# Gate and up products of a SwiGLU FFN by one level of Strassen's algorithm, and no sums of SBUF tiles on GpSimd

## The chip, the cores and the metric

One Trainium2 chip, one of its cores. The metric is the device time of one execution in microseconds (us), lower is better; the time before is the median of three runs. TensorE is written PE, its weight loads PEld, VectorE DVE, ScalarE ACT, GpSimd POOL, and the queue from which the loads are issued SP.

## The reference

A trunk of two layers on 512 tokens of width 1024, all in f32. Each layer is a token mixer (layer 0: forgetting attention and sparse attention; layer 1: differential attention), a cross attention to 256 memory tokens, and a SwiGLU FFN of inner width 2816, each between two RMS norms with a residual. What the change touches is the FFN:

```python
def swiglu(h, wg, wu, wd):
    return (jax.nn.silu(h @ wg) * (h @ wu)) @ wd
...
        y = swiglu(rms_norm(x, g[4]), ffn_wg[layer], ffn_wu[layer], ffn_wd[layer])
        x = x + rms_norm(y, g[5])
```

## The kernel before

**Splitting.** Every f32 operand of a large product is kept as a high part in the float32r type and a low part, the rest. `split` makes them from a source: an ACT copy writes the high part, a DVE subtraction the low part. `mm` then issues three matmuls for one 128-row block of the contraction: high by high, high by low, low by high.

**FFN (`ffn`).** The inner width of 2816 is cut into 22 chunks of 128 columns. `up(c)` loads 512 KB of the gate weights and 512 KB of the up weights (tiles `raw`, 3 buffers), splits each into two tiles `w` (8 buffers), and for each of the two weights issues 8 `mm`, one per 128 rows of the contraction: the weights are the stationary operand, and the transposed tokens `hT` (high and low, `[128, 8, 512]`) stream by, 512 columns to a matmul. That is 48 matmuls for a chunk; for the first two chunks they come in two halves of 256 tokens (96 matmuls), since the last token blocks are late. Then silu and the product: `th` by ACT's tanh, two `scalar_tensor_tensor` of DVE, and a split of the result into `acts[c]`, whose low part is a subtraction on GpSimd. The down product takes groups of three chunks (the last group four): for each of 4 token blocks and 2 column halves one PSUM bank gets 3 matmuls per chunk (512 columns each), and DVE adds the bank to `yacc`. The weights `wd` of a chunk are one more load of 512 KB and one more split of 1024 columns. Buffers: 8 PSUM banks `ps`, 20 tiles `u` of 1024 columns (`unit`), 10 tiles `q` of 512 columns (`qtile`).

**The end of a mixer (`last_heads`, `chain`).** For each block of 128 tokens: output projection, `post_norm` (a sum of squares on ACT, a power on GpSimd, products and sums on DVE and GpSimd), cross attention, a second `post_norm`, and `norm_T`: the norm ahead of the FFN, eight PE transposes into two banks, and a split of each bank into `hT`. In `post_norm` the first half's sum goes to GpSimd and the second half's to DVE.

**The order.** Nothing is issued where it stands in the code. `Plan` records every operation with what it reads and writes; `forward` simulates the engines with a price for each operation and writes one fixed order for each engine, `backward` works out priorities from it, 14 rounds of both, and the order with the shortest simulated end is issued. A PSUM bank counts as one region for dependences. When DVE is busy and GpSimd free, `lend` hands a waiting `tensor_add`, `tensor_sub` or `tensor_mul` on SBUF tiles from DVE to GpSimd. Because all operations are issued in one place, every row of the profile has the line 491, and operations are told apart by their tiles.

Of the kernel before, what the change touches and what calls it, by code (L numbers as in the profile page):

```python
# [19 lines left out]
P = 128  # L20
# [5 lines left out]
DH = 64  # L26
# [8 lines left out]
LEAD = 2  # L35
KA = 6
ROWS = slice(0, DH), slice(DH, P)
ORDER = 0, 4, 5, 6, 7, 1, 8, 9, 10, 11, 12, 13, 2, 3
# [49 lines left out]
class Plan:  # L88
# [11 lines left out]
    ALPHA, BETA = 1.0, 2.0  # L100
    FLEX, MORE, HOLD = 100.0, 1.5, 5000.0

# [31 lines left out]

    def note(self, eng, method, args, kw):
        aps = [("out" if i == 0 else "in", v) for i, v in enumerate(args) if isinstance(v, bass.AP)]
# [36 lines left out]
        return op  # L173
# [8 lines left out]
    def price(self, eng, method, args, kw, aps):  # L182
# [6 lines left out]
        if eng == "tensor":  # L189
            if method == "transpose":  # L190
                return 107.0
            c = self.free(args[2]) / 2.4
            return max(25.0, 2.5 + (c if args[2].dtype == F32R else 4 * c))
        if eng == "scalar":
            extra = sum(isinstance(kw.get(k), bass.AP) for k in ("bias", "scale", "accum_out"))
            return (52 if aps[1].space == PSUM else 95) + 0.83 * n + 93 * extra
        if eng == "vector":
# [4 lines left out]
            if method in ("tensor_copy", "tensor_scalar", "memset") and not psum:  # L202
                return 65 + 0.52 * n
            return 65 + 1.04 * n
        if eng == "gpsimd":
            if method == "tensor_tensor":
                return 260 + 200 * n
            if method in ("tensor_sub", "tensor_add", "tensor_mul"):
                return 100 + 2.3 * n
            if method == "memset":  # L210
                return 30 + 0.84 * n
            return (322 if len(aps) > 3 else 222) + 0.84 * n
        raise ValueError(method)

    def order(self):
        ops = self.ops
        n = len(ops)
        self.eng0 = [o["eng"] for o in ops]
        self.succ = [[] for _ in range(n)]
# [15 lines left out]
        self.span, self.at, self.fin, out = best[:4]  # L235
        self.eng = best[5]
        return out

    def backward(self, run):

        span, at, fin, out, reuse, eng = run
        ops, n = self.ops, len(self.ops)
        pred = [list(o["deps"]) for o in ops]
# [14 lines left out]
        while ev:  # L258
# [5 lines left out]
            for e in engines:  # L264
                h = ready[e]
                while h and busy[e] <= now + 1e-9:
                    i = heapq.heappop(h)[1]
                    cost = ops[i]["cost"] if eng[i] == self.eng0[i] else ops[i]["alt"][eng[i]]
                    end = now + cost
# [14 lines left out]
    def forward(self, prio, far):  # L284

        ops, eng, succ = self.ops, list(self.eng0), self.succ
        n = len(ops)
# [109 lines left out]

        def lend(e, f):

            wait = busy[e] - now  # L400
            for top, i in sorted(ready[e]):
                c = ops[i]["alt"].get(f)
                if c and wait > self.MORE * (c - ops[i]["cost"]) \
                        and not any(at[j] < now + c and prio[j] < top + self.HOLD for j in soon[f]):
                    ready[e].remove((top, i))
                    heapq.heapify(ready[e])
                    eng[i] = f
                    heapq.heappush(ready[f], (top, i))
                    return
                wait += ops[i]["cost"]  # L410

        while done < n:
# [21 lines left out]
            while again:  # L434
                again = False
                if busy["gpsimd"] <= now + 1e-9 and not ready["gpsimd"] and busy["vector"] > now:
                    lend("vector", "gpsimd")
                for e, heap in ready.items():
                    while heap and busy[e] <= now + 1e-9:
# [11 lines left out]
                        done += 1  # L451
                        cost = o["cost"] if e == self.eng0[i] else o["alt"][e]
                        if o["dma"]:
# [31 lines left out]
        return max(ends), at, ends, out, reuse, eng  # L485

# [7 lines left out]
class Trunk:  # L494
# [13 lines left out]

    def mm(self, ps, L, R, first, last):
        (lh, ll), (rh, rl) = L, R  # L510
        mmul = self.nc.tensor.matmul
        mmul(ps, lh, rh, start=first, stop=False)
        mmul(ps, lh, rl, start=False, stop=False)
        mmul(ps, ll, rh, start=False, stop=last)

# [116 lines left out]
    def norm_T(self, src, g, dst, tb):  # L632
# [5 lines left out]
        self.turn(hs, dst, tb)  # L638

    def hT_tiles(self):  # L640
        return [self.tile([P, KO, T], F32R, f"hT{k}") for k in ("hi", "lo")]

    def post_norm(self, ys, g, x, tb):
# [205 lines left out]
    def chain(self, tb, c):  # L849
# [85 lines left out]
        if c["hT"] is None:  # L935
            c["hT"] = self.hT_tiles()
        self.norm_T(self.xhalves(x, tb), c["g"][2], c["hT"], tb)
        yield
# [26 lines left out]
    def last_heads(self, l, w, units, n, c, x_src, fill):  # L965
# [20 lines left out]
        def rest():  # L986
# [8 lines left out]
              *[(block(tb), [max(ready[tb], LATE + tb) + STAGE * s if s < 5 else max(ready[tb] + STAGE * s, LATE + tb + STAGE * s, ready[3] + 0.2 if s > 4 else 0) for s in range(9)]) for tb in range(NT)])  # L995
        return c["x"], c["hT"]


    def ffn(self, l, x, hT):
        nc, a = self.nc, self.a  # L1000
        groups = [list(range(c, min(c + 3, NCH))) for c in range(0, NCH - 1, 3)]
        groups[-1].append(NCH - 1)
        acts = {}

        def up(c):
# [4 lines left out]
            for s in parts:  # L1010
                for ps, wf in ((pg, wg), (pu, wu)):
                    for ko in range(KO):
                        self.mm(ps[:, s], wf(ko), (hT[0][:, ko, s], hT[1][:, ko, s]), ko == 0, ko == KO - 1)
            th, b = self.qtile(), self.qtile()
            nc.scalar.activation(th, pg, AF.Tanh, scale=0.5)
# [8 lines left out]
        up(0)  # L1024
        for gi, grp in enumerate(groups):
            last = gi == len(groups) - 1
            for c in grp[1:]:
                up(c)
            wds = []
# [5 lines left out]
            else:  # L1035
                up(groups[gi + 1][0])
            if yacc is None:
# [556 lines left out]
    def run(self):  # L1594
# [3 lines left out]
        self.xsave = tc.nc.dram_tensor("xsave", (T, D), F32, kind="Internal").ap()  # L1598
        x, hT = self.mixer0(x)
        blocks = self.ffn(0, x, hT)  # L1600
        x, hT = self.mixer1(x, blocks)
        for tb in self.ffn(1, x, hT):
            for c in (slice(0, 512), slice(512, 1024)):
# [42 lines left out]
```

## Time and profile before

| what | value |
|---|---|
| time, median of 3 runs | 1422.42 us (1422.35 to 1424.1) |
| the profiled execution's own time | 1422.67 us |
| its span, first to last instruction | 1421.0 us |
| PE busy | 1383.2 us, 97% of the span |
| DVE busy | 833.7 us, 59% |
| ACT busy | 725.0 us, 51% |
| GpSimd busy | 355.9 us, 25% |
| mean share of time that the 16 DMA engines are busy | 30.2% on the queue of the loads |

The span is the profiled execution's, and 1.67 us of that execution's time lies outside it. Matmuls overlap in the pipe, so a row's duration of a matmul (390 ns at 512 columns) is longer than the distance from one start to the next; the distance is what a stream of them costs. The same holds in a small way for DVE and ACT. A row of the timeline merges neighbours of one kind: its first number is the start, the second the time from the first start to the last end.

### The profile page before, as it was taken

What the parts mean: (1) busy time and instruction counts of PE and PEld (TensorE: products, weight loads), DVE (VectorE), ACT (ScalarE), POOL (GpSimd) and SP (SyncE); (2) the same over time, 40 slices, a digit from 0 to 9 for tenths busy, and PEclk for the clock granted to TensorE, in tenths of its full rate; (3) what the DMA queues carried; (4) which work ended last, traced back from release to release, by engine and by line L of the source; (5) the groups of instructions that cost most, each with busy time, mean ns of one, the idle gap of its engine ahead of it and who ended that gap; (6) DMA issues with size and microseconds to landing.
All of it is one profiled execution on the core that took longest, in us unless ns stands there. A gap on an engine that the chain in (4) does not pass through costs nothing.

```text
span 1421.0 us, 21566 instructions
## 1 busy us (share of the span) xinstructions
PE 1383.2 (97%) x8003; PEld 1204.0 (85%) x8003; DVE 833.7 (59%) x1851; ACT 725.0 (51%) x1606; POOL 355.9 (25%) x429
## 2 busy tenths in 40 slices
PE   7999999999899999999999999999989999999997
PEld 6788988889788888888889999988878888888886
DVE  5667899498842333433466888876984233343344
ACT  5768879488643122223245677786863322222322
POOL 2203334244320121012031233312552012101202
PEclk9999999999999999999999999999999999999999
DMA  7251112321233233324321321243234323332411
GB/s 218 65 150 47 46 45 87 107 74 61 89 119 89 89 104 90 114 78 134 105 74 54 95 91 61 77 147 104 85 92 121 89 84 110 89 108 85 119 60 60
DMA packets 150425, 132.05 MB, mean 93 GB/s; under 512 B 6928, under 2 KB 134096, under 8 KB 150320
## 3 DMA queue, kind: packets, MB, share of 16 engines
q1 hardware_dynamic: 150320, 130.67, 30.2%
q8 instruction: 63, 1.03, 0.3%
q14 instruction: 42, 0.34, 0.1%
HBM read 126.26 MB, written 4.19 MB: 92 GB/s over the span
## 4 chain that ended last, share of the span: by engine, by line
PE 84%; DVE 7%; ACT 3%; DMA 2%; POOL 2%; issue 2%; SPq 0%; POOLq 0%; DVEq 0%; ACTq 0%
PE ps L491 84%; DVE q L491 2%; DVE x L491 1%; DVE u L491 1%; ACT q L491 1%; DVE c L491 1%; DMA raw<-in_ev_w_in_dram 1%; POOL c L491 1%; POOL q L491 1%; ACT u L491 1%; DVE pt L491 1%; DMA pt<-in_ev_w_in_dram 0%; DVE w L491 0%; ACT pt L491 0%; POOL x L491 0%
## 5 line engine op out<-in xcount | busy, mean ns | idle before, releaser
L491 PE MATMUL ps<-hThi,w 128*128 128x512 f32 (+1 forms) x1664 | 488.0, 375 | 2.6 <-DVE q L491 2.6
L491 PEld LDWEIGHTS ps<-hThi,w 128*128 128x128 f32 x1664 | 306.5, 190 | 58.3 <-ACT junk L491 1.6
L491 PE MATMUL ps<-hTlo,w 128*128 128x512 f32 (+1 forms) x832 | 311.6, 375 | 0.4 <-DVE hTlo L491 0.2
L491 PE MATMUL ps<-w,hThi 128*128 128x256 f32 (+2 forms) x1280 | 281.9, 316 | 2.3 <-ACT hThi L491 2.3
L491 DVE TENSOR_TENSOR w<-raw,w 128x1024 fp32r<-128x1024 f32 (+1 forms) x136 | 170.2, 1268 | 152.3 <-issue 72.8
L491 ACT ACTIVATE w<-raw 128x1024 fp32r<-128x1024 f32 (+1 forms) x153 | 158.4, 1051 | 164.4 <-PE ps L491 138.7
L491 PE MATMUL ps<-pt,u 128*128 128x512 f32 (+3 forms) x1126 | 231.8, 338 | 1.4 <-DVE pt L491 0.8
L491 PEld LDWEIGHTS ps<-w,hThi 128*128 128x128 f32 x1280 | 210.5, 192 | 15.2 <-ACT hThi L491 3.2
L491 DVE TENSOR_TENSOR u<-ps,u 128x512 f32<-128x512 f32 (+6 forms) x278 | 150.6, 546 | 116.4 <-PE ps L491 98.0
L491 PEld LDWEIGHTS ps<-pt,u 128*128 128x128 f32 (+1 forms) x1126 | 175.2, 173 | 31.6 <-DVE pt L491 1.5
L491 POOL TENSOR_TENSOR u<-q,u 128x512 fp32r<-128x512 f32 x44 | 64.0, 1454 | 542.7 <-ACT u L491 542.7
L491 PE MATMUL ps<-w,hTlo 128*128 128x256 f32 (+2 forms) x640 | 199.8, 313 | 0.0
L491 PE MATMUL ps<-u 128*128 128x512 f32 (+4 forms) x806 | 186.4, 348 | 0.1
L491 PEld LDWEIGHTS ps<-hTlo,w 128*128 128x128 f32 x832 | 158.0, 190 | 28.3 <-DVE hTlo L491 1.3
L491 PEld LDWEIGHTS ps<-u 128*128 128x128 f32 (+1 forms) x806 | 131.1, 183 | 18.4 <-DVE pt L491 0.4
L491 DVE SCALAR_TENSOR_TENSOR q<-q,ps 128x512 f32<-128x512 f32 x88 | 60.3, 686 | 141.1 <-PE ps L491 103.5
L491 ACT ACTIVATE u<-ps 64x256 fp32r<-64x256 f32 (+6 forms) x269 | 116.0, 438 | 51.8 <-PE ps L491 47.4
L491 ACT ACTIVATE q<-ps 128x256 f32<-128x256 f32 (+6 forms) x158 | 72.7, 460 | 119.0 <-PE ps L491 117.4
L491 PEld LDWEIGHTS ps<-w,hTlo 128*128 128x128 f32 x640 | 122.4, 192 | 7.2 <-DVE hTlo L491 0.8
L491 PE MATMUL ps<-ident,q 128*128 128x128 f32 (+1 forms) x645 | 109.6, 278 | 18.0 <-DVE q L491 13.8
L491 PEld LDWEIGHTS ps<-ident,q 128*128 128x128 f32 (+1 forms) x645 | 77.5, 141 | 28.3 <-DVE q L491 11.5
L491 ACT ACTIVATE q<-q,c 128x128 f32<-128x128 f32 (+3 forms) x160 | 88.7, 557 | 12.7 <-DVE c L491 11.8
(151 smaller groups left out, 1518.1 us busy)
## 6 DMA issues: line engine op xcount, KB each, us to landing
raw<-in_ffn_wg_dram SPq DMA_DIRECT2D x44, 512.0 KB
raw<-in_ffn_wu_dram SPq DMA_DIRECT2D x44, 512.0 KB
raw<-in_ffn_wd_dram SPq DMA_DIRECT2D x44, 512.0 KB
raw<-in_od_w_in_dram SPq DMA_DIRECT2D x24, 512.0 KB
raw<-in_ev_w_in_dram SPq DMA_DIRECT2D x16, 512.0 KB
u<-in_sandwich_g_dram SPq DMA_DIRECT2D x10, 512.0 KB
x<-in_x_dram SPq DMA_DIRECT2D x8, 512.0 KB
raw<-in_ev_w_out_dram SPq DMA_DIRECT2D x8, 512.0 KB
```

The lines of the kernel that those rows point to most:

```text
L491: getattr(getattr(self.nc, self.eng[i]), method)(*args, **kw)
```

## The change

**The products.** For chunks 2 to 21 of each FFN (`PLAIN = 2`), gate and up weights are seen as one 2 by 2 block matrix: B11 and B21 are the upper and lower 512 rows of the gate chunk, B12 and B22 those of the up chunk; the tokens are A11, A12 (tokens 0 to 255, first and second half of the width), A21, A22 (tokens 256 to 511). Seven block products in place of eight give both results (Winograd's form of Strassen's algorithm). A block product is 4 `mm` = 12 matmuls of 256 columns. The sums of weights (`t1` to `t4`) are four DVE operations of 512 columns, and each of the seven right operands is split by itself (7 splits of 512 columns in place of 2 of 1024), into one `w` tile for high and low. The sums of products are formed in PSUM where a product can accumulate onto an earlier one (`lead` keeps the accumulating product apart for the planner, `skip_group_check` goes to the matmul); between them stand three ACT copies and three DVE additions of 256 columns.

**The token sums.** `norm_S` takes the place of `norm_T` ahead of the FFN: it keeps the f32 values of the first two blocks in two tiles `u` (`keep`), and for blocks 2 and 3 forms S1, S2, S4 and splits them into six more tiles `u`. S3 is split by `third()` ahead of chunk 2 into the part of `hT` that held A21.

**GpSimd.** `lend` goes, and so do the GpSimd sums in `post_norm` and in `finish`; all of them are on DVE. GpSimd keeps the powers, the scalings and the memsets.

**The planner's prices.** Matmuls, transposes and operations on 64 partitions get other prices; nothing else of the planner changes.

```diff
+PLAIN = 2
+HALF_ROWS = 115
...
-        if method == "matmul" and not kw["start"]:
+        if method == "matmul" and not (kw["start"] or lead):
             op["group"] = self.last_group[args[0].tensor.name]
...
-        op["alt"] = {}
-        if eng.name == "vector" and method in ("tensor_sub", "tensor_add", "tensor_mul") and op["cost"] > self.FLEX \
-                and all(ap.space != PSUM for _, ap in aps):
-            op["alt"]["gpsimd"] = self.price("gpsimd", method, args, kw, [v for _, v in aps])
-        op["load"] = 53.0 if method != "matmul" else self.free(args[1]) / (1.2 if args[1].dtype == F32R else 2.4)
+        op["load"] = 53.0 if method != "matmul" else self.free(args[1]) / 2.4
...
-                return 107.0
+                return 109.0
             c = self.free(args[2]) / 2.4
-            return max(25.0, 2.5 + (c if args[2].dtype == F32R else 4 * c))
+            return max(25.0, (13.0 if c > 100 else 6.5) + (c if args[2].dtype == F32R else 4 * c))
...
-                if busy["gpsimd"] <= now + 1e-9 and not ready["gpsimd"] and busy["vector"] > now:
-                    lend("vector", "gpsimd")
...
+    def norm_S(self, src, g, c, tb):
...
+            if tb < 2:
+                nc.scalar.activation(keep[i], pt, AF.Copy)
+            pts.append(pt)
+        if tb < 2:
+            return
...
+        nc.scalar.activation(a21, pts[0], AF.Copy)
+        nc.vector.tensor_add(s1, pts[1], a21)
+        nc.vector.tensor_sub(s2, s1, keep[0])
+        nc.vector.tensor_sub(keep[0], keep[0], a21)
+        nc.vector.tensor_sub(keep[1], keep[1], s2)
+        cs = slice((tb - 2) * P, (tb - 1) * P)
+        for n, t in ((1, s1), (2, s2), (4, keep[1])):
+            hi, lo = c["S"][n]
+            self.split(hi[:, :, cs], lo[:, :, cs], t.rearrange("p (a b) -> p a b", b=P))
...
-                (nc.vector if i else nc.gpsimd).tensor_add(x[tb][:, s], x[tb][:, s], h)
+                nc.vector.tensor_add(x[tb][:, s], x[tb][:, s], h)
             else:
-                (nc.vector if i else nc.gpsimd).tensor_mul(ys[i], ys[i], g[:, s])
+                nc.vector.tensor_mul(ys[i], ys[i], g[:, s])
...
-            nc.gpsimd.tensor_sub(at[:, 512:1024], b, at[:, 0:512].bitcast(F32))
+            nc.vector.tensor_sub(at[:, 512:1024], b, at[:, 0:512].bitcast(F32))
+
+        def third():
+
+            for i in range(2):
+                cs = slice(i * P, (i + 1) * P)
+                hi, lo = blocks["S3"]
+                self.split(hi[:, :, cs], lo[:, :, cs], ops["keep"][i][:, 0:512].rearrange("p (a b) -> p a b", b=P))
+
+        def fast(c):
...
+            (b11, b21), (b12, b22) = [(r[:, 0:512], r[:, 512:1024]) for r in raw]
+            t1, t2, t3, t4 = [self.qtile() for _ in range(4)]
+            nc.vector.tensor_sub(t1, b12, b11)
+            nc.vector.tensor_sub(t2, b22, t1)
+            nc.vector.tensor_sub(t3, b22, b12)
+            nc.vector.tensor_sub(t4, b21, t2)
+            G, U, W = self.bank(), self.bank(), self.bank()[:, 0:256]
+            G0, G1, U0, U1 = G[:, 0:256], G[:, 256:512], U[:, 0:256], U[:, 256:512]
+
+            def product(ps, left, right, first):
+                wt = self.tile([P, 1024], F32R, "w", 8)
+                hi, lo = wt[:, 0:512], wt[:, 512:1024]
+                self.split(hi, lo, right)
+                ah, al = blocks[left]
+                for k in range(4):
+                    s = slice(k * P, (k + 1) * P)
+                    self.mm(ps, (hi[:, s], lo[:, s]), (ah[:, k, :], al[:, k, :]), first and k == 0, k == 3,
+                            not first and k == 0, skip_group_check=not first)
+
+            product(G0, "A11", b11, True)
+            product(U0, "S2", t2, True)
+            copies, w7 = self.qtile(), self.qtile()[:, 0:256]
+            p1, u2 = copies[:, 0:256], copies[:, 256:512]
+            nc.scalar.activation(p1, G0, AF.Copy)
+            nc.vector.tensor_add(U0, U0, p1)
+            nc.scalar.activation(u2, U0, AF.Copy)
+            product(W, "S3", t3, True)
+            nc.scalar.activation(w7, W, AF.Copy)
+            product(G0, "A12", b21, False)
+            product(U0, "S1", t1, False)
+            nc.vector.tensor_add(U1, U0, w7)
+            product(W, "A22", t4, False)
+            product(U0, "S4", b22, False)
+            nc.vector.tensor_add(G1, W, u2)
+            finish(c, G, U)
```

## Rows read from the trace of the kernel before

**Rows 1.** The page: busy time of each engine, share of the span, instructions.

```profile
PE 1383.2 (97%) x8003; PEld 1204.0 (85%) x8003; DVE 833.7 (59%) x1851; ACT 725.0 (51%) x1606; POOL 355.9 (25%) x429
```

**Rows 2.** Busy time by stretch (columns in the first row).

```profile
core 0: us, PE busy (x) PEld busy (x) DVE busy (x) ACT busy (x) POOL busy (x), PEclk, DMA share, GB/s
...
390.00:560.00 170.00, 170.00 (x793) 142.62 (x793) 63.92 (x71) 53.72 (x67) 26.08 (x15) 1.00 0.34 100
...
1000.00:1060.00 60.00, 53.28 (x422) 47.87 (x421) 52.73 (x94) 49.78 (x132) 34.17 (x40) 1.00 0.26 80
```

**Rows 3.** What PE waited for: us in total, times, longest.

```profile
PE ps L491 <- DVE q L491: 16.4, 9, 7.5
...
PE ps L491 <- DVE hTlo L491: 0.2, 1, 0.2
```

**Rows 4.** Timeline of PE in FFN 0, matmuls of 512 columns.

```profile
473.29 1.52 PE L491 MATMUL ps<-pt,u 128*128 128x512 f32 x6
474.65 0.84 PE L491 MATMUL ps<-u 128*128 128x512 f32 x3
475.33 1.52 PE L491 MATMUL ps<-pt,u 128*128 128x512 f32 x6
...
488.02 0.62 PE L491 MATMUL ps<-hThi,w 128*128 128x512 f32 x2
...
488.70 0.62 PE L491 MATMUL ps<-hThi,w 128*128 128x512 f32 x2
```

**Rows 5.** Timeline of PE at the start of FFN 0, matmuls of 256 columns.

```profile
382.80 0.40 PE L491 MATMUL ps<-hThi,w 128*128 128x256 f32 x2
383.04 0.28 PE L491 MATMUL ps<-hTlo,w 128*128 128x256 f32 x1
383.16 0.40 PE L491 MATMUL ps<-hThi,w 128*128 128x256 f32 x2
```

**Rows 6.** Timeline of DVE, operations back to back.

```profile
118.06 0.68 DVE L491 TENSOR_TENSOR x<-ps,q 64x512 f32<-64x512 f32 x1
118.67 1.16 DVE L491 TENSOR_TENSOR pt<-ps,pt 128x512 fp32r<-128x512 f32 x2
...
475.53 0.69 DVE L491 TENSOR_TENSOR u<-ps,u 128x512 f32<-128x512 f32 x1 [0.21 <-PE ps L491]
...
498.42 2.36 DVE L491 TENSOR_TENSOR w<-raw,w 128x1024 fp32r<-128x1024 f32 x2 [2.94 <-PE ps L491]
```

**Rows 7.** Groups of DVE by form, whole span: busy us, mean ns, idle before.

```profile
L491 DVE TENSOR_TENSOR u<-ps,u 128x512 f32<-128x512 f32 x103 | 70.9, 690 | 98.1 <-PE ps L491 98.0
...
L491 DVE TENSOR_TENSOR u<-ps,u 128x256 fp32r<-128x256 f32 x20 | 8.4, 420 | 2.1 <-ACT u L491 2.0
...
L491 DVE TENSOR_TENSOR x<-x,u 128x512 f32<-128x512 f32 x4 | 2.7, 676 | 0.0
```

**Rows 8.** Groups of ACT by form, whole span.

```profile
L491 ACT ACTIVATE q<-ps 128x256 f32<-128x256 f32 x56 | 21.3, 381 | 29.5 <-PE ps L491 28.6 <-POOL q L491 0.2
L491 ACT ACTIVATE u<-q 128x512 fp32r<-128x512 f32 x44 | 27.5, 624 | 50.6 <-DVE q L491 50.6
```

**Rows 9.** Groups of GpSimd by form, whole span.

```profile
L491 POOL TENSOR_TENSOR u<-q,u 128x512 fp32r<-128x512 f32 x44 | 64.0, 1454 | 542.7 <-ACT u L491 542.7
L491 POOL TENSOR_TENSOR w<-raw,w 128x1024 fp32r<-128x1024 f32 x17 | 51.3, 3015 | 30.7 <-issue 20.1 <-PE ps L491 10.6
```

**Rows 10.** The chain of waits just before FFN 0: start, us, what.

```profile
366.74 2.92 POOL x L491 x2
...
370.41 1.47 POOL c L491
```

**Rows 11.** Busy time by stretch over the start of FFN 0.

```profile
370.00:380.00 10.00, 8.19 (x44) 7.79 (x45) 9.12 (x15) 5.63 (x12) 4.17 (x4) 0.66 0.46 149
380.00:410.00 30.00, 29.91 (x212) 27.98 (x211) 17.05 (x19) 12.99 (x17) 3.75 (x3) 1.00 0.43 127
```

More of the change, by code (lines that the diff above doesn't have):

```diff
@@ L135, in note @@
     def note(self, eng, method, args, kw):
+        lead = kw.pop("lead", False)
         aps = [("out" if i == 0 else "in", v) for i, v in enumerate(args) if isinstance(v, bass.AP)]
@@ L190, in price @@
             if method == "transpose":
-                return 107.0
+                return 109.0
             c = self.free(args[2]) / 2.4
-            return max(25.0, 2.5 + (c if args[2].dtype == F32R else 4 * c))
+            return max(25.0, (13.0 if c > 100 else 6.5) + (c if args[2].dtype == F32R else 4 * c))
+        half = HALF_ROWS if eng in ("scalar", "vector") and n > 100 and aps[0].ap[0][1] == DH else 0
         if eng == "scalar":
             extra = sum(isinstance(kw.get(k), bass.AP) for k in ("bias", "scale", "accum_out"))
-            return (52 if aps[1].space == PSUM else 95) + 0.83 * n + 93 * extra
+            return (52 if aps[1].space == PSUM else 95) + 0.83 * n + 93 * extra + half
         if eng == "vector":
@@ L203, in price @@
                 return 65 + 0.52 * n
-            return 65 + 1.04 * n
+            return 65 + 1.04 * n + half
         if eng == "gpsimd":
@@ L217, in order @@
         n = len(ops)
-        self.eng0 = [o["eng"] for o in ops]
+        self.eng = [o["eng"] for o in ops]
         self.succ = [[] for _ in range(n)]
@@ L235, in order @@
         self.span, self.at, self.fin, out = best[:4]
-        self.eng = best[5]
         return out
     def backward(self, run):
-        span, at, fin, out, reuse, eng = run
-        ops, n = self.ops, len(self.ops)
+        span, at, fin, out, reuse = run
+        ops, eng, n = self.ops, self.eng, len(self.ops)
         pred = [list(o["deps"]) for o in ops]
@@ L284, in forward @@
     def forward(self, prio, far):
-        ops, eng, succ = self.ops, list(self.eng0), self.succ
+        ops, eng, succ = self.ops, self.eng, self.succ
         n = len(ops)
@@ L396, in pick @@
             return found
[L398 to L410, printed above, removed]
         while done < n:
@@ L484, in forward @@
                                 seq += 1
-        return max(ends), at, ends, out, reuse, eng
+        return max(ends), at, ends, out, reuse
     def issue(self, tc):
@@ L507, in tile, with mm @@
         return self.nc.tile(self.sb, shape, dtype, tag, bufs)
-    def mm(self, ps, L, R, first, last):
+    def mm(self, ps, L, R, first, last, lead=False, **kw):
         (lh, ll), (rh, rl) = L, R
         mmul = self.nc.tensor.matmul
-        mmul(ps, lh, rh, start=first, stop=False)
-        mmul(ps, lh, rl, start=False, stop=False)
-        mmul(ps, ll, rh, start=False, stop=last)
+        mmul(ps, lh, rh, start=first, stop=False, lead=lead, **kw)
+        mmul(ps, lh, rl, start=False, stop=False, **kw)
+        mmul(ps, ll, rh, start=False, stop=last, **kw)
     def unit(self, dtype=F32R):
@@ L638, in norm_T @@
         self.turn(hs, dst, tb)
+    def norm_S(self, src, g, c, tb):
+        nc = self.nc
+        r = self.rstd(src)
+        hs = [self.qtile() for _ in range(2)]
+        for i in range(2):
+            nc.vector.scalar_tensor_tensor(hs[i], src[i], r, g[:, i * 512:(i + 1) * 512], op0=ALU.mult, op1=ALU.mult)
+        if tb < 2:
+            c["keep"].append(self.unit(F32))
+        keep = [c["keep"][tb % 2][:, i * 512:(i + 1) * 512] for i in range(2)]
+        pts = []
+        for i in range(2):
+            pt = self.bank()
+            for j in range(4):
+                nc.tensor.transpose(pt[:, j * P:(j + 1) * P], hs[i][:, j * P:(j + 1) * P], self.ident)
+            sl = (slice(None), slice(i * 4, i * 4 + 4), slice(tb * P, (tb + 1) * P))
+            self.split(c["hT"][0][sl], c["hT"][1][sl], pt.rearrange("p (a b) -> p a b", b=P))
+            if tb < 2:
+                nc.scalar.activation(keep[i], pt, AF.Copy)
+            pts.append(pt)
+        if tb < 2:
+            return
+        if tb == 2:
+            c["S"] = {n: [self.unit().rearrange("p (k t) -> p k t", k=4) for _ in range(2)] for n in (1, 2, 4)}
+        a21, s1, s2 = [self.qtile() for _ in range(3)]
+        nc.scalar.activation(a21, pts[0], AF.Copy)
[7 more added lines that the diff above has]
+            self.split(hi[:, :, cs], lo[:, :, cs], t.rearrange("p (a b) -> p a b", b=P))
     def hT_tiles(self):
@@ L936, in chain @@
             c["hT"] = self.hT_tiles()
-        self.norm_T(self.xhalves(x, tb), c["g"][2], c["hT"], tb)
+            c["keep"] = []
+        self.norm_S(self.xhalves(x, tb), c["g"][2], c, tb)
         yield
@@ L1019, in up @@
             nc.scalar.activation(at[:, 0:512], b, AF.Copy)
-            nc.gpsimd.tensor_sub(at[:, 512:1024], b, at[:, 0:512].bitcast(F32))
+            nc.vector.tensor_sub(at[:, 512:1024], b, at[:, 0:512].bitcast(F32))
+        def third():
+            for i in range(2):
+                cs = slice(i * P, (i + 1) * P)
+                hi, lo = blocks["S3"]
+                self.split(hi[:, :, cs], lo[:, :, cs], ops["keep"][i][:, 0:512].rearrange("p (a b) -> p a b", b=P))
+        def fast(c):
+            rows = lambda w: w[l].rearrange("(ko p) c -> p ko c", p=P)[:, :, c * P:(c + 1) * P]
+            raw = []
+            for w in ("ffn_wg", "ffn_wu"):
+                raw.append(self.tile([P, 1024], F32, "raw", 3))
+                self.loads.append(nc.sync.dma_start(raw[-1].rearrange("p (k c) -> p k c", c=P), rows(a[w])))
+            (b11, b21), (b12, b22) = [(r[:, 0:512], r[:, 512:1024]) for r in raw]
[31 more added lines that the diff above has]
+            finish(c, G, U)
@@ L1022, in ffn, with make @@
+        def make(c):
+            if c == PLAIN:
+                third()
+            (up if c < PLAIN else fast)(c)
         where = self.pt_tiles
         yacc = None
-        up(0)
+        make(0)
         for gi, grp in enumerate(groups):
@@ L1035, in ffn @@
             else:
-                up(groups[gi + 1][0])
+                make(groups[gi + 1][0])
             if yacc is None:
@@ L1598, in run @@
         self.xsave = tc.nc.dram_tensor("xsave", (T, D), F32, kind="Internal").ap()
[L1599 to L1602, printed above, removed]
+        x, ops = self.mixer0(x)
+        blocks = self.ffn(0, x, ops)
+        x, ops = self.mixer1(x, blocks)
+        for tb in self.ffn(1, x, ops):
             for c in (slice(0, 512), slice(512, 1024)):
```

19 lines of the change are left out of this document (11 added, 8 removed).

## The prediction

> **What bounds the kernel now.** I read the page first: PE is busy in 97% of the span, no other engine in more than 59% [rows 1]. A busy PE could still be a waiting PE, since matmul ends are modelled, so the list of what PE waited for came next: eleven rows, from 16.4 us down to 0.2 us, 29.5 us in all, of 1421 [rows 3]. The table by stretch then says where slack lies: inside an FFN PE is busy without a break while DVE has 63.92 of 170 us, ACT 53.72 and GpSimd 26.08; at the end of a mixer DVE is at 52.73 of 60 us [rows 2]. So time taken off PE's stream of matmuls inside an FFN comes off the end, as long as DVE keeps up; what is put on DVE at the end of a mixer or just behind it may show.
>
> The timeline gives the price of PE. In the down product nine matmuls of 512 columns go from 473.29 to 475.33, in the up product three from 488.02 to 488.70: 0.2267 us each, in both [rows 4]. The first two chunks of an FFN already run at 256 columns with a weight load each, which is the shape the change uses: three from 382.80 to 383.16, 0.120 us each [rows 5]. That is at the full clock (granted 1.00); over 370 to 380 us the mean is 0.66, between the two levels 1.2 and 2.4 GHz, after PE had stood still in the norms [rows 10, 11].
>
> **The change part by part.**
>
> *Products on PE.* A chunk falls from 48 matmuls of 512 columns, 48 x 0.2267 = 10.88 us, to 7 x 12 = 84 of 256, 84 x 0.120 = 10.08 us. That is 0.80 us, where the columns alone (24,576 against 21,504, an eighth) would give 1.36. 20 chunks in 2 FFNs: 40 x 0.80 = **-32.0 us**. Chunks 0 and 1 and the down product (24 x 0.2267 = 5.44 us a chunk) stay. A chunk with its down product goes from 16.32 to 15.52 us.
>
> The Trainium skill, "TensorE: Matmul & The Clock Gate", section "Back-to-back issue gap", gives for a stream of pairs of load and matmul 81 ns at 128 columns and 131 ns at 512. An estimate on the line between them is 98 ns at 256; by it a chunk would go from 48 x 131 = 6.3 to 84 x 98 = 8.2 us, and 40 chunks would lose 77 us. This trace differs at 512 columns by far (226.7 ns) and at 256 (120 ns), so the measurement decides.
>
> *DVE in a fast chunk.* Prices are distances between starts: 0.61 us for 512 columns (118.06 to 118.67), 1.14 for 1024 (the second of two that take 2.36, the first taken as 1.22) [rows 6]; for 256 columns, which no such pair shows, the duration 0.42 [rows 7]. Before: three splits of 1024, two `scalar_tensor_tensor`, and the additions into `yacc` (6 groups of 7 have 8 each, 48 / 22 = 2.2 a chunk): 3.42 + 1.22 + 1.33 = 5.97 us of 16.32, 37%; the row says 63.92 / 170 = 38% [rows 2], so the count is right. After: four weight sums, seven low parts, two `scalar_tensor_tensor` and the subtraction that comes from GpSimd are 14 x 0.61 = 8.54; three additions of 256 are 1.26; one split of 1024 is 1.14; `yacc` 1.33. Sum 12.27 of 15.52 us, 79%. With the durations (0.68 to 0.69 [rows 7]) in place of the distances it would be 13.6 us, 88%. By either count DVE stays below PE. No cost, then, but the cover shrinks from 10.4 to between 1.9 and 3.3 us a chunk.
>
> *ACT in a fast chunk.* Seven high parts of 512 from SBUF at 0.624, three copies of 256 from PSUM at 0.381 [rows 8], tanh and the high part of the result taken at 0.624 too, the 1024 of `wd` at twice that: 8.0 us, half of the chunk. No cost.
>
> *New waits of PE inside a chunk.* PE runs in order, and a bank is one region. The product S1 into U waits for: product S2 done, DVE's addition of `p1`, ACT's copy `u2`. DVE starts 0.20 us after the last matmul (475.33, 475.53 [rows 4, 6]); with two more hops taken as the same, 3 x 0.20 + 0.42 + 0.38 = 1.40 us. Two products stand between, 24 x 0.120 = 2.88 us: 1.48 us to spare. Product S4 waits for DVE's addition into U1: 2 x 0.20 + 0.42 = 0.82 against one product, 1.44: 0.62 to spare. One operation of 0.61 ahead of it on DVE fits, one of 1.14 is 0.52 too late, and one of those comes per chunk. Behind a waiting PE stands the rest of the chunk. I take 0.05 us a chunk, **+2.0 us**; below, nothing; above, the rival on DVE.
>
> *Loads.* Three of 512 KB a chunk as before, with DMA at a share of 0.34 [rows 2]. But the two `raw` tiles of a chunk are now held until B22 is split last, and the `w` tiles give 8 products of lead, not 2 chunks. Eight products are 11.5 us of PE, more than a chunk's 10.08. No cost.
>
> *Token sums.* For blocks 2 and 3 `norm_S` adds four sums and three low parts on DVE, 7 x 0.61 = 4.3 us each, and `third` two: 2 x 4.3 + 1.2 = 9.8 us an FFN. The place is the start: DVE has 30 - 17.05 = 12.95 us free between 380 and 410 [rows 11], before the first fast chunk is through. In the same stretch that chunk wants 12.27 - 5.97 = 6.3 us more. 16.1 against 12.95 is 3.1 us too much; since S1 and S4 are needed only by the fifth and seventh product, I charge 2.0 an FFN, **+4.0 us**. Bounds: nothing, and everything (below). The eight extra `u` tiles, of 20, can hold up a block's transposes here; no row prices that, and it is part of the upper bound.
>
> *Sums taken from GpSimd.* Inside the FFN the 44 subtractions of 1.45 us [rows 9] are in DVE's count. The 17 weight splits lent to GpSimd (3.0 us each) are 17 x 1.14 = 19.4 us of DVE over the whole span, which has 587 us free [rows 1]. At the end of a mixer, `post_norm` puts 8 sums, 4.9 us, on a DVE that is at 88% [rows 2]. Against that, the chain just before the FFN ran through two of these sums on GpSimd, 2.92 us, and then a power of 1.47 [rows 10]; two on DVE are 1.22, so up to 1.7 us an FFN come back. Taken as **0**; bounds -3.4 and +9.8.
>
> *Prices of the planner.* They only change the order. All that any order could win on PE's waits is 29.5 us [rows 3]. Taken as 0; I allow 4 us either way.
>
> Sum: -32.0 + 2.0 + 4.0 = -26.0 us. The profiled execution took 1422.67 (span 1421.0 and 1.67 around it), 0.25 above the median of the runs; 1422.42 - 26.0 = **1396.5 us**, a ratio of 0.982.
>
> **The rivals.**
>
> *Nothing is given back.* The order hides the sums and the chain through GpSimd gets shorter: 1422.4 - 32.0 - 3.4 = 1387, or 1383 with the 4 us of the new prices. For it: DVE idle in every FFN stretch. Against: DVE at 88% where the FFN starts.
>
> *The start of the FFN is exposed.* DVE saturated, PE waits for S2, S3 or `hT`. In full 9.8 + 4.9 = 14.7 us an FFN: 1422.4 - 32.0 + 2.0 + 29.4 = 1422, no change. Half of it: 1407. For it: 9.12 of 10 us on DVE at 370 to 380 [rows 11]. Against: PE has 11.5 us of chunks 0 and 1 (96 x 0.120) left once `hT` is whole, and needs S2 only then.
>
> *DVE's queue, the other side.* If DVE lags behind the written order by one operation of 1.14 and one of 0.61 in each chunk, PE waits 1.75 - 1.48 = 0.27 us ahead of S1 and 1.75 - 0.62 = 1.13 ahead of S4, 1.4 us a chunk: 1422.4 - 32.0 + 4.0 + 56 = 1450 us. From (32.0 - 4.0) / 40 = 0.70 us a chunk on, the change loses. For it: DVE at 79 to 88%, in order, with the order fixed from other prices than the chip's. Against: before, DVE had no such lag anywhere in an FFN, since PE did not wait at all there.
>
> *The matmul's fixed part.* 226.7 and 120.0 ns give (2 x 120.0 - 226.7) = 13.3 ns a matmul beside its columns. If the new operands made that 36 ns, 129.5 ns a matmul, 84 of them would cost the 10.88 us of before, and with the 6 us above the time would be 1428. For it: 84 weight loads against 48. Against: the rows at 256 columns [rows 5] are those very loads. The Trainium skill's distances named above would be the extreme of this rival.
>
> **How the numbers follow.** Forecast 0.63, with a range of its own of 1388 to 1406 (a stall of 0 to 0.25 us a chunk, a start of 0 to 4 us an FFN). Nothing given back 0.12. Start exposed by half or more 0.14, of which 0.02 reach no change. DVE's queue 0.08. Fixed part 0.03, of which 0.01 no change. About 0.2%, 2.8 us, is what a measurement of this kernel can tell from no change. Faster 0.87, same 0.03, slower 0.10. The range 1383 to 1411 leaves out the two last rivals and the worse part of the exposed start, some 2 in 10.
>
> **What would show it.** Right: three matmuls every 0.36 us in chunks 2 to 21 at a granted clock of 1.00; PE busy without a break there; DVE at 79 to 88% of the FFN stretches, ACT near 50%; GpSimd almost idle there; the distance from one group of down products to the next 46.6 us in place of 49.0. Wrong: rows of PE waiting for DVE `ps` or `u`, or ACT `q`, repeated in each chunk (DVE's queue); a gap of PE ahead of chunk 2 or later transposes at the end of a mixer (the start); a distance above 0.39 us for three matmuls (fixed part); or mixers whose own stretches grow, since DVE lost GpSimd's help there.

## The result and the profile after

The changed kernel takes **1385.68 us** (median of 4 runs, 1383.51 to 1389.33); the kernel before took 1423.26 beside it (4 runs, 1422.35 to 1424.13). The ratio is 0.9739, with a 95% interval of 0.9716 to 0.9761: 37.6 us less, where the forecast was 26.0 less and the range reached down to 1383. The profiled execution took 1385.17 us, with a span of 1383.4.

The page of the kernel after, busy time, share of the span and instructions of each engine, answers to [rows 1] (its rows have the line 470; the other kernels below have 469, 489 or 493):

```profile
PE 1352.8 (98%) x9443; PEld 1247.4 (90%) x9443; DVE 1114.9 (81%) x2485; ACT 861.1 (62%) x1954; POOL 200.0 (14%) x307
```

PE is busy for 30.4 us less, although it issues 1,440 matmuls more. DVE goes from 59 to 81% of the span and GpSimd from 25 to 14%. Two stretches inside the two FFNs, and behind them the start of FFN 0, answer to [rows 2, 11] (columns as there):

```profile
400.00:700.00 300.00, 300.00 (x2098) 281.78 (x2097) 244.41 (x399) 147.85 (x264) 1.86 (x2) 1.00 0.38 112
1060.00:1360.00 300.00, 299.11 (x2086) 280.73 (x2085) 241.25 (x395) 144.88 (x259) 0.00 (x0) 1.00 0.34 102
```

```profile
380.00:410.00 30.00, 28.60 (x216) 27.20 (x215) 29.54 (x47) 20.96 (x36) 0.00 (x0) 1.00 0.30 89
```

Inside an FFN PE has next to no break, DVE stands at 81% (244.41 of 300) and ACT at 49%. At the start DVE is full, 29.54 of 30 us, and PE stands still for 1.40, waiting for parts of `hT`. The timeline of PE in a fast chunk, matmuls of 256 columns, answers to [rows 5]:

```profile
420.56 1.60 PE L470 MATMUL ps<-u,w 128*128 128x256 f32 x12
422.00 0.28 PE L470 MATMUL ps<-hThi,w 128*128 128x256 f32 x1
...
463.60 1.55 PE L470 MATMUL ps<-pt,u 128*128 128x512 f32 x6
...
510.18 1.55 PE L470 MATMUL ps<-pt,u 128*128 128x512 f32 x6
```

Twelve matmuls, one product, go from 420.56 to 422.00: 0.120 us each. One group of down products starts at 463.60 and the next at 510.18: 46.58 us for three chunks. What PE waited for over the whole span answers to [rows 3] (us in total, times, longest):

```profile
PE ps L470 <- DVE q L470: 10.6, 5, 7.6
...
PE ps L470 <- DVE ps L470: 0.4, 1, 0.4
```

All thirteen rows together are 23.4 us, 29.5 before. The wait that the rival on DVE's queue needs, for DVE's additions into a bank, occurs once.

Where the 37.6 us lie, by the distance from the first matmul of an FFN to the first of the next mixer, and so on (profiled executions, us):

| kernel | mixer 0 | FFN 0 | mixer 1 | FFN 1 | tail |
|---|---|---|---|---|---|
| before | 370.74 | 363.00 | 315.13 | 364.71 | 7.42 |
| after | 368.19 | 349.39 | 309.16 | 349.87 | 6.79 |
| difference | -2.55 | -13.61 | -5.97 | -14.84 | -0.63 |

The border between FFN 0 and mixer 1 is not at the same work in both kernels. Of the 528 matmuls of FFN 0's down product, 24 come behind that border before and 12 after:

```profile
740.28 1.65 PE L491 MATMUL ps<-pt,u 128*128 128x512 f32 x6
741.77 1.54 PE L491 MATMUL ps<-u 128*128 128x512 f32 x6
...
748.92 1.55 PE L491 MATMUL ps<-pt,u 128*128 128x512 f32 x6
750.30 1.52 PE L491 MATMUL ps<-u 128*128 128x512 f32 x6
```

```profile
723.69 1.64 PE L470 MATMUL ps<-pt,u 128*128 128x512 f32 x6
725.17 1.54 PE L470 MATMUL ps<-u 128*128 128x512 f32 x6
```

At 0.2267 us each that is 5.4 and 2.7 us. Counted to FFN 0, they make it 16.3 us shorter in place of 13.6, and mixer 1 only 3.3. So the two FFNs give 31.2 us, and the mixers and the tail 6.4. The forecast had all of its 26.0 at the FFNs, and nothing for the rest.

### The profile page after: what moved, and what is told of

Same layout as the page of the kernel before. It is cut to its first block, busy times and chain, and to the rows that moved or that the text cites. A ratio compares the mean times of both kernels' runs of the same rounds, so it can differ in the third digit from the quotient of the medians.

```text
span 1383.4 us, 25460 instructions
## 1 busy us (share of the span) xinstructions
PE 1352.8 (98%) x9443; PEld 1247.4 (90%) x9443; DVE 1114.9 (81%) x2485; ACT 861.1 (62%) x1954; POOL 200.0 (14%) x307
## 4 chain that ended last, share of the span: by engine, by line
PE 84%; DVE 8%; ACT 2%; issue 2%; DMA 2%; POOL 1%; SPq 0%; POOLq 0%; DVEq 0%; ACTq 0%
PE ps L470 84%; DVE q L470 2%; DVE u L470 1%; DVE x L470 1%; DVE w L470 1%; POOL c L470 1%; DVE pt L470 1%; ACT q L470 1%; DMA raw<-in_ffn_wu_dram 1%; ACT junk L470 1%; DVE c L470 1%; DVE hTlo L470 1%; DMA x<-in_x_dram 0%; DMA raw<-in_od_w_in_dram 0%; ACT u L470 0%
## 5 line engine op out<-in xcount | busy, mean ns | idle before, releaser
L470 PE MATMUL ps<-hThi,w 128*128 128x256 f32 (+1 forms) x1664 | 338.4, 292 | 1.7 <-ACT hThi L470 1.2
L470 PE MATMUL ps<-hTlo,w 128*128 128x256 f32 (+1 forms) x832 | 242.2, 292 | 2.4 <-DVE hTlo L470 2.4
L470 DVE TENSOR_TENSOR w<-raw,w 128x512 fp32r<-128x512 f32 (+2 forms) x193 | 170.3, 887 | 31.6 <-ACT w L470 27.4
L470 PE MATMUL ps<-u,w 128*128 128x256 f32 x1440 | 192.9, 283 | 0.4 <-DVE ps L470 0.4
L470 ACT ACTIVATE w<-raw 128x512 fp32r<-128x512 f32 (+2 forms) x193 | 148.5, 786 | 68.8 <-DMA raw<-in_ffn_wg_dram 24.7
L470 ACT ACTIVATE q<-ps 128x256 f32<-128x256 f32 (+5 forms) x282 | 118.3, 428 | 112.1 <-PE ps L470 96.3
L470 PEld LDWEIGHTS ps<-u,w 128*128 128x128 f32 x1440 | 181.8, 192 | 1.4 <-DVE ps L470 0.9
L470 ACT ACTIVATE u<-ps 64x256 fp32r<-64x256 f32 (+5 forms) x277 | 120.5, 442 | 51.1 <-PE ps L470 47.6
L470 ACT ACTIVATE w<-q 128x512 fp32r<-128x512 f32 x160 | 99.9, 629 | 48.4 <-PE ps L470 22.7
L470 DVE TENSOR_TENSOR w<-q,w 128x512 fp32r<-128x512 f32 x160 | 107.9, 686 | 21.2 <-ACT w L470 20.5
```

The source lines that it names most:

```text
L470: getattr(getattr(self.nc, self.eng[i]), method)(*args, **kw)
```

## The experiments

The theory on seeing this: the products give about the 30 us forecast, and the surplus comes from the sums that GpSimd no longer does. Rivals: the surplus comes from the new prices and the order they make; or the products themselves give more than 0.80 us a chunk. All medians below stand beside 1422.1 to 1422.9 us for the kernel before, on the same chip as each.

**What the sums on GpSimd cost in the kernel before.** `no_gpsimd_sums` puts all sums on DVE and changes nothing else of before; the three runs behind it do one part each.

```diff
-                if busy["gpsimd"] <= now + 1e-9 and not ready["gpsimd"] and busy["vector"] > now:
-                    lend("vector", "gpsimd")
...
-                (nc.vector if i else nc.gpsimd).tensor_add(x[tb][:, s], x[tb][:, s], h)
+                nc.vector.tensor_add(x[tb][:, s], x[tb][:, s], h)
...
-                (nc.vector if i else nc.gpsimd).tensor_mul(ys[i], ys[i], g[:, s])
+                nc.vector.tensor_mul(ys[i], ys[i], g[:, s])
...
-            nc.gpsimd.tensor_sub(at[:, 512:1024], b, at[:, 0:512].bitcast(F32))
+            nc.vector.tensor_sub(at[:, 512:1024], b, at[:, 0:512].bitcast(F32))
```

> The kernel before with nothing changed but that no sum of SBUF tiles goes to GpSimd (no lending, post_norm and the low part of the FFN's product on DVE). Theory A (prices): no change, 1420 to 1425 us. Theory B (GpSimd): the chain ahead of each FFN is shorter and the mixers gain, 1412 to 1416. Theory C (order): within 5 us, either sign. If DVE at the end of the mixers were the limit it would be slower, up to 1432.

> The kernel before without the planner's lending alone (17 weight splits of 3.0 us, 28 rope operations and some sums go back to DVE); GpSimd keeps post_norm's sums and the FFN's 44 low parts. Taking all sums off GpSimd gave 11.8 us. Theory A, DVE and GpSimd slow each other, so the 51 us of lent weight splits matter: 5 to 8 us faster, 1414 to 1417. Theory B, the chain of the norms is what counts: no change, 1420 to 1424.

> The kernel before with only post_norm's sums moved from GpSimd to DVE (2 per token block and layer, 1.3 us each on GpSimd, ahead of the power in its queue, and one per block at each FFN's end). Theory A (DVE and GpSimd slow each other): 1 to 2 us, 1420 to 1422. Theory B (the chain of the norms): 5 to 8 us, 1414 to 1417, and the low clock at the start of FFN 0 goes. My bound in the prediction was 3.4 us.

> The kernel before with only the 44 low parts of the FFN's product moved from GpSimd to DVE. PE did not wait inside the FFN, so both theories say no change, 1420 to 1424, but for the last chunk's low part, on the way to the last down products: 0.8 us an FFN at most.

| part taken from GpSimd | us | ratio (95%) |
|---|---|---|
| all three | 1410.52 | 0.9915 (0.9902 to 0.9929) |
| `lend` alone | 1413.11 | 0.9937 (0.9925 to 0.9949) |
| the sums of `post_norm` alone | 1425.15 | 1.0022 (1.0013 to 1.0031) |
| the low parts of `finish` alone | 1422.80 | 1.0002 (0.9993 to 1.0010) |

So GpSimd's help cost the kernel before 11.8 us, and 9.0 of them come with `lend` alone. The low parts cost nothing that can be told from noise. The sums of `post_norm` taken away alone make it 3.0 slower, so the parts don't add up: 9.0 - 3.0 - 0.7 is 5.3, not 11.8. Each of these kernels also has an order of its own, and the new prices, with nothing else changed, move the kernel before by 5.0 us (below); how much of each row is the order's was not separated.

Two things in the trace go with the gain. DVE's own operations become shorter; two forms, kernel before and then `no_gpsimd_sums` (groups by form, whole span):

```profile
L491 DVE TENSOR_TENSOR w<-raw,w 128x1024 fp32r<-128x1024 f32 x133 | 167.4, 1276 | 150.5 <-issue 72.8 <-PE ps L491 56.3 <-ACT w L491 11.3
L491 DVE SCALAR_TENSOR_TENSOR q<-x,c,u 128x512 f32<-128x512 f32 x32 | 28.5, 918 | 4.2 <-POOL c L491 4.0
```

```profile
L489 DVE TENSOR_TENSOR w<-raw,w 128x1024 fp32r<-128x1024 f32 x150 | 181.9, 1224 | 92.7 <-PE ps L489 75.1 <-ACT w L489 13.1 <-ACT q L489 3.5
L489 DVE SCALAR_TENSOR_TENSOR q<-x,c,u 128x512 f32<-128x512 f32 x32 | 22.5, 747 | 2.6 <-POOL c L489 2.5
```

And the low clock at the start of FFN 0 [rows 11] is gone; `no_gpsimd_sums`, then `no_lending`, over the same 10 us:

```profile
370.00:380.00 10.00, 10.00 (x84) 9.60 (x82) 8.02 (x14) 4.00 (x10) 1.54 (x2) 1.00 0.17 53
```

```profile
370.00:380.00 10.00, 10.00 (x83) 9.60 (x82) 8.71 (x15) 5.41 (x10) 3.78 (x3) 1.00 0.32 106
```

A granted clock of 1.00 there, the level of 2.4 GHz, against a mean of 0.66, and PE busy for 10.00 of 10 us against 8.19. FFN 0 is 4.3 us shorter than before in `no_gpsimd_sums` (358.74), FFN 1 1.3 (363.40), and the two mixers 3.1 and 2.9. Of the 12.1 us between the two spans, 8.5 are PE standing idle for less, 6.3 of them in the mixers. In FFN 0 PE is also busy for 3.1 us less with the same products, about what the low clock cost: 10 us at 0.66 do the work of 6.6 at full clock (before, then `no_gpsimd_sums`):

```profile
370.74:733.74 363.00, 361.45 (x1684) 303.06 (x1682) 151.37 (x179) 108.01 (x147) 62.71 (x39) 0.99 0.35 105
```

```profile
367.63:726.37 358.74, 358.30 (x1681) 300.54 (x1681) 171.18 (x212) 108.30 (x148) 7.01 (x8) 1.00 0.35 105
```

**The prices.** `prices` gives before the new prices and nothing else; `no_gpsimd_sums_and_prices` does both; `strassen_old_prices` is the kernel after with the old ones.

The edit of the last, against the kernel after:

```diff
-        op["load"] = 53.0 if method != "matmul" else self.free(args[1]) / 2.4
+        op["load"] = 53.0 if method != "matmul" else self.free(args[1]) / (1.2 if args[1].dtype == F32R else 2.4)
...
-                return 109.0
+                return 107.0
...
-            return max(25.0, (13.0 if c > 100 else 6.5) + (c if args[2].dtype == F32R else 4 * c))
-        half = HALF_ROWS if eng in ("scalar", "vector") and n > 100 and aps[0].ap[0][1] == DH else 0
+            return max(25.0, 2.5 + (c if args[2].dtype == F32R else 4 * c))
...
```

> The kernel before with nothing changed but the planner's prices (matmul, weight load, transpose, operations on 64 partitions). After the change the stretches outside the FFNs were 9.1 us shorter by the trace, which the prediction had taken as 0. Theory A, the order follows the better prices: most of it comes here, 1412 to 1416 us. Theory B, it comes from the sums taken off GpSimd: no change here, 1420 to 1425. Theory C, any new order moves the mixers by some us either way: a change of unforeseen sign, at most 5 us.

> The kernel before with both, all of the change but Strassen's products and token sums. Theories A and B both say 1412 to 1416 us (8 to 10 below before), so that the products alone are worth 26 to 30 us; if A and B add up, 1408 to 1412. Theory C: anywhere within 5 us of before, and the products then are worth 33 to 42.

> The changed kernel with the planner's old prices. Theory A (prices): the 9 us are lost, 1393 to 1397 us. Theory B (GpSimd): as the changed kernel, 1384 to 1388. The old price of a matmul is 10.5 ns too low for every matmul, 0.9 us in 84 of them, so a rival says that the order inside a fast chunk goes wrong too, with PE waiting for DVE in each chunk: 1400 or more.

The prices cost time wherever they were tried: 1427.34 against 1422.30 for before (ratio 1.0037, 1.0025 to 1.0050), 1411.98 against 1410.52 without GpSimd's sums, and 1385.68 against **1379.04** (ratio to before 0.9693, 0.9680 to 0.9707) with the products. So `strassen_old_prices` is faster than both kernels, and the rival of the prices falls: they took 6.6 us off the gain. The last two stand on different chips, but the runs of `strassen_old_prices` (1378.15 to 1379.47) all lie below those of the kernel after (1383.51 to 1389.33). FFN 0 as one stretch, first in the kernel after, then in `strassen_old_prices`:

```profile
368.19:717.58 349.39, 346.58 (x2414) 324.37 (x2413) 291.04 (x472) 177.82 (x324) 8.24 (x8) 1.00 0.37 109
```

```profile
366.26:714.00 347.74, 347.61 (x2427) 326.40 (x2426) 292.86 (x476) 180.29 (x331) 8.31 (x9) 1.00 0.36 108
```

PE's idle time there is 2.81 us with the new prices and 0.13 with the old. With the old ones all 528 down matmuls of FFN 0 stand ahead of its border; counted alike, FFN 0 is 4.4 us shorter with them, mixer 0 1.9 and FFN 1 0.9, and mixer 1 is 1.3 longer. Which of the prices does it was not tried.

**The token sums and the products, one by one.** `PLAIN = 22` leaves no fast chunk but forms the token sums; `PLAIN = 12` makes 10 chunks of each FFN fast. Both stand on the kernel after.

```diff
-PLAIN = 2
+PLAIN = 22
```

> The changed kernel with every chunk in the plain form: the token sums of norm_S are made and never used, the products are those of before. Against the kernel with neither token sums nor products (1412.0 us): the prediction charges 4.0 us for the sums less third's share, 1414 to 1417 us. If they are hidden, 1410 to 1413. If the start is exposed, 1420 or more.

> The changed kernel with Strassen's form in chunks 12 to 21 only, 10 an FFN in place of 20. If the products pay 0.80 us a chunk, 20 chunks less cost 16.0 us: 1400 to 1403 us. If part of the gain were in the order or the start, less: 1390 to 1397. If fast chunks give back 0.2 us each in waits of PE: 1397 to 1399.

1416.15 and 1399.69 us (ratios 0.9954, 0.9941 to 0.9966, and 0.9838, 0.9825 to 0.9852). Against 1411.98 without token sums the sums cost 4.2 us. The 20 chunks 12 to 21 of both FFNs then give 16.5 us, 0.82 each, and the 20 earlier ones 14.0, 0.70 each. All 40 give 30.5 us, 0.76 each. Not all of that lies in the FFNs. Between the spans of `token_sums_only` and after, 29.4 us, 26.3 lie in the FFNs with the down matmuls counted alike, 0.66 a chunk (0.73 in the late chunks, 0.59 in the early ones), and 3.1 in the mixers and the tail, where the products change only the order.

**How much room DVE has.** `dve_4_more_sums` forms `t1` five times, four sums of 512 columns more in each fast chunk.

```diff
-            nc.vector.tensor_sub(t1, b12, b11)
+            for _ in range(5):
+                nc.vector.tensor_sub(t1, b12, b11)
```

> The changed kernel (1385.7 us) with the first weight sum of each fast chunk done five times in place of once: four more DVE operations of 512 columns a chunk, with the same result. By distances between starts DVE has 12.27 + 4 x 0.61 = 14.7 of 15.5 us a chunk: no or little cost, 1385 to 1393. By the rows' durations it has 13.6 + 2.7 = 16.3: DVE is the bound, 0.8 us a chunk, 1417 or more.

1392.30 us (ratio 0.9790, 0.9776 to 0.9803), 6.6 more than after, 0.17 a chunk if all of it lay there; of the 6.0 us between the two spans 3.4 lie in the FFNs. The stretch of the FFN and two waits of PE in it:

```profile
400.00:700.00 300.00, 298.69 (x2087) 280.05 (x2086) 286.82 (x475) 146.53 (x262) 1.85 (x2) 1.00 0.37 111
```

```profile
467.26 1.69 PE L470 MATMUL ps<-u,w 128*128 128x256 f32 x12 [0.29 <-DVE ps L470]
490.79 1.69 PE L470 MATMUL ps<-u,w 128*128 128x256 f32 x12 [0.95 <-DVE ps L470]
```

By distances DVE's chunk is then 12.27 + 4 x 0.61 = 14.71 us, under PE's 15.52; by durations it is 13.6 + 4 x 0.69 = 16.36, and 0.84 us a chunk would have made some 34 us. The distances count, and even at a busy share of 96% the order hides nearly all of it.

**The products beside GpSimd's sums.** `strassen_gpsimd_kept` puts the products and token sums into the kernel before, with its prices, with `lend` and all sums of GpSimd. `strassen_low_part_gpsimd` is `strassen_old_prices` with only the 44 low parts of `finish` back on GpSimd:

```diff
-            nc.vector.tensor_sub(at[:, 512:1024], b, at[:, 0:512].bitcast(F32))
+            nc.gpsimd.tensor_sub(at[:, 512:1024], b, at[:, 0:512].bitcast(F32))
```

> Strassen's products and token sums alone, on the kernel before with its old prices and all its GpSimd sums, lending too. If the parts add up: 1422.3 less 31.5 (old prices with and without Strassen: 1410.5 to 1379.0), 1389 to 1393 us. If lending to GpSimd hurts more where DVE is at 80%: 1394 or more. If GpSimd's help is needed there: below 1388.

> Strassen with the old prices and no lending (1379.0 us), but the 44 low parts of the FFN's product back on GpSimd, 1.4 us each, one per chunk; DVE is relieved by 0.61 us a chunk. Theory A, DVE operations with both inputs in SBUF wait while GpSimd reads SBUF: each low part holds DVE up by up to 1.4 us, a net 0.8 us a chunk on DVE, 13.1 of 15.5; PE then waits little, 1379 to 1386. Theory D, any GpSimd sum beside a DVE at 80% stops PE: 1390 or more. If GpSimd simply helped: 1377 to 1379.

With all of GpSimd's sums: **1431.80 us**, slower than before (ratio 1.0072, 1.0056 to 1.0088). With the low parts alone: 1381.18 (0.9712, 0.9699 to 0.9726). Against 1379.04 without any, GpSimd's sums cost 52.8 us, and the low parts alone only 2.1, which is not clear of the noise (the intervals of the two ratios overlap). So the cost comes with `lend` and the sums of `post_norm`, or with all three together; they were not tried one by one here. The profiled execution of `strassen_gpsimd_kept` took 1437.83 us, the slowest of its six (the others 1430.43 to 1432.41), 58.6 more than that of `strassen_old_prices`. With the down matmuls counted alike, 22.7 and 18.9 of them lie in the FFNs, 6.6 and 9.9 in the mixers. What PE waited for, and a stretch of FFN 0:

```profile
PE ps L493 <- DVE ps L493: 19.3, 14, 3.5
...
PE ps L493 <- DVE hTlo L493: 7.6, 5, 3.4
```

```profile
400.00:730.00 330.00, 315.85 (x2156) 294.33 (x2155) 263.56 (x351) 154.53 (x277) 98.02 (x66) 0.98 0.36 104
```

One of those waits, on three engines: DVE, GpSimd, PE.

```profile
420.16 0.67 DVE L493 SCALAR_TENSOR_TENSOR q<-q,ps 128x512 f32<-128x512 f32 x1
...
421.82 1.78 DVE L493 TENSOR_TENSOR w<-raw,w 128x512 fp32r<-128x512 f32 x1
423.52 1.77 DVE L493 TENSOR_TENSOR q<-raw,q 128x512 f32<-128x512 f32 x1
425.21 1.75 DVE L493 TENSOR_TENSOR w<-raw,w 128x512 fp32r<-128x512 f32 x1
426.89 0.68 DVE L493 TENSOR_TENSOR q<-raw,q 128x512 f32<-128x512 f32 x1
427.49 0.42 DVE L493 TENSOR_TENSOR ps<-ps,q 128x256 f32<-128x256 f32 x1
```

```profile
420.04 1.30 POOL L493 TENSOR_TENSOR u<-q,u 128x512 fp32r<-128x512 f32 x1 [1.89 <-ACT u L493]
421.30 1.75 POOL L493 TENSOR_TENSOR q<-raw 128x512 f32<-128x512 f32 x1
423.00 1.73 POOL L493 TENSOR_TENSOR u<-q,u 128x512 fp32r<-128x512 f32 x1
424.70 1.71 POOL L493 TENSOR_TENSOR w<-raw,w 128x512 fp32r<-128x512 f32 x1
```

```profile
427.96 2.93 PE L493 MATMUL ps<-u,w 128*128 128x256 f32 x12 [3.54 <-DVE ps L493]
```

While GpSimd works through three sums of 512 columns, each of DVE's takes 1.75 to 1.78 us; the next one, alone, takes 0.68. The three take 5.07 us from 421.82 to 426.89 in place of 3 x 0.61, 3.2 us late; the addition into U comes at 427.49, and PE, which stood before the last product of the chunk, S4, goes on at 427.96. Its twelve matmuls then take 2.93 us where 1.60 is usual: after 3.54 us of standing still the granted clock is 0.50, the level of 1.2 GHz:

```profile
427.90:431.00 3.10, 3.04 (x13) 3.04 (x14) 2.89 (x7) 1.01 (x2) 0.00 (x0) 0.50 0.88 244
```

In 420 to 690 us DVE's sums of two SBUF tiles average 1057 ns for `w<-raw,w` (686 in the kernel after) and 1223 for `q<-raw` (687), while its additions with a PSUM operand stay at 422 (426). All 14 waits for DVE's additions lie in the FFNs, each of them before an S4; an S1 waited once, for ACT (`q`, 2.15 us).

## Why the prediction was right, and where it was off

The medians make a chain. Its links were not all timed on one chip; the kernel before gave 1422.30 to 1423.26 beside them, and the four runs of the kernel after spread over 5.8 us, so a step is good to some 1 to 3 us. It is one order of the parts: they are not independent, and in another order they have other sizes (with the products in place the sums taken from GpSimd give 52.8 us in place of 11.8, and the prices cost 6.6 in place of 1.5).

| step | from | to | measured | forecast |
|---|---|---|---|---|
| sums taken from GpSimd | 1422.30 | 1410.52 | -11.8 | 0 (-3.4 to +9.8) |
| prices | 1410.52 | 1411.98 | +1.5 | 0 (-4 to +4) |
| token sums | 1411.98 | 1416.15 | +4.2 | +4.0 |
| products, with waits in a chunk | 1416.15 | 1385.68 | -30.5 | -32.0 + 2.0 = -30.0 |

*The sum.* The forecast is 1396.4 us by its own terms. The measured time lies in the range of 1383 to 1411, but 2.3 us below the 1388 to 1406 that the prediction gave its own forecast. The products and the token sums came out near their sizes, both in part by luck, and the 11.6 us that are missing are about the size of the one term taken as 0, the sums taken from GpSimd.

*Products.* Right in mechanism: 0.120 us for a matmul of 256 columns in the fast chunks as in the first two, and 46.58 us from group to group where 46.6 was forecast, so 0.80 us a chunk in the middle of an FFN. The rival of the matmul's fixed part did not happen. The distances that "TensorE: Matmul & The Clock Gate", section "Back-to-back issue gap", in the Trainium skill would have made (98 ns at 256 columns by the prediction's estimate) are not seen either. That the whole step comes to 30.5 is in part luck: the FFNs give 26.3 of 29.4 us by the traces, less than forecast, and the mixers, where nothing was forecast, 3.1.

*DVE and ACT.* DVE at 81% lies in the 79 to 88% worked out, ACT at 49% near half, and PE without a break. Of the two counts of DVE the one by distances was right, as the four sums more show.

*Waits in a chunk.* 0.05 us a chunk was charged. The trace of after shows one wait for DVE's additions, 0.4 us. What the products lose in the FFNs they lose for the most part at the start: PE's idle time in the two FFN stretches is 1.30 us in `token_sums_only`, 1.47 in `half_the_chunks`, where the first fast chunk is chunk 12, and 4.57 in after, of which 3.1 are waits for parts of `hT`. DVE is busy for 29.54 of the 30 us from 380 in after, for 25.77 in `half_the_chunks`. So a DVE too full at the start, the reason given for the token sums, is real, but it shows in the step of the products, and the early chunks give less than the late ones.

*Token sums.* 4.2 us against 4.0, but not from the place forecast. Of the 3.1 us between the profiled executions of `token_sums_only` and `no_gpsimd_sums_and_prices` (1414.51 and 1411.45), 2.2 lie in mixer 0, ahead of the FFN's first matmul (369.23 against 367.03), and 0.3 and 0.5 in the FFNs. That the size came out is therefore in part luck; whether the sums or the changed order do it there is open.

*Sums taken from GpSimd.* This is the term that was mis-sized: taken as 0, with -3.4 as the lower bound, it measured -11.8. It counted what the moved sums would cost DVE and what the short chain ahead of the FFN would give back, and left out what GpSimd's sums did to DVE's others while both ran. The rows of before hint at it: `w<-raw,w` at 1276 ns in the mean, 1224 without GpSimd's sums (fences above). By the traces about 3 of the 12 us are the low clock at the start of FFN 0, which goes away with `lend`, and 8.5 are PE standing idle for less. That PE stood idle because GpSimd slowed DVE is shown beside the products only, in the rows at 421.82; here it is the likely reason, and the change of order is a rival that no run excludes.

*Prices.* Inside its bound here, +1.5; with the products in place they cost 6.6, more than the 4 us allowed. "They only change the order" was right, and the order is worse; why was not settled.

*The rivals.* Nothing given back (1383 to 1387) has the nearest time, by luck and not for its reason: the token sums and the prices were paid, and GpSimd's sums gave more than they cost. DVE's queue is real: where GpSimd keeps its sums, the waits stand where they were described, before S4, though not in every chunk: 14 in 40, 19.3 us. With waits at the start and the lower clock the FFNs lose 41.6 us, 1.04 a chunk against the 1.4 worked out and the 0.70 from which it decides, and the time ends on the other side of before. The order is written with 0.60 us for a sum of 512 columns (65 + 1.04 x 512 ns, the planner's price), and beside GpSimd it takes 1.75. Without those sums it stays away; the two halves of this change belong together. The products without the other half lose 9.7 us, the other half alone gains 11.8, and both with the old prices gain 43.

## What to carry to other kernels

Before sums go to a second engine because it is idle, look at what the first engine's rows take while both run: a kernel bound by PE paid 11.8 us for such help with DVE at 59%, and 52.8 with DVE at 81%. A trade of matmuls for additions is priced by the measured distance of the smaller matmul (0.80 us a chunk here, where the columns alone promise 1.36), and by whether the engine that adds keeps its distance, not its busy share, below PE's. When an edit carries several parts, run each of them without the others: here the part with new prices was a loss inside a gain.

## What the runs showed of the hardware

A sum of two SBUF tiles of 512 columns takes DVE 0.68 us alone and 1.75 to 1.78 beside such a sum on GpSimd, which in turn goes from 1.30 to between 1.71 and 1.75. The pair advances every 1.70 us (421.82, 423.52, 425.21), nearer to one behind the other (0.61 + 1.30 = 1.91) than to both at once (1.30). DVE's operations with one operand in PSUM keep their time: 422 ns against 426 in the mean for 256 columns, and 0.67 us for the one of 512 at 420.16, which runs beside the sum of GpSimd at 420.04. The Trainium skill, "SBUF — State Buffer", section "Who interferes with whom", says that a DVE instruction with two SBUF inputs contends with a GpSimd instruction that reads SBUF, since its second input comes through an interface that both share; the rows agree, for the operation with one PSUM operand too.

DVE could be busy for 286.82 of 300 us, and PE still lost only 1.31 us there. Rows of DVE back to back overlap, 0.68 us long at a distance of 0.61, so their summed durations (16.36 us for a chunk of 15.52) ask for more than DVE needs.
